# One decoder layer on one core: a re-ordered first phase, sample states updated in the MLP phase, and a fixed order for the last block

## The chip, the core and the metric

The kernel runs on one core of one Trainium2 chip. Every time is in device microseconds (us). The time of the kernel before is the median of three runs; the profile and the trace are those of one further execution of the same program.

## The reference

One step of one decoder layer (width 2048) is computed for two streams: a prompt of 256 tokens and 8 sample tokens that each carry recurrent states from the past. All arithmetic is float32.

```python
mod = silu(c) @ w_ada + b_ada                      # 6 x 2048 columns
h = rmsnorm(x, g_pre_mix) * (1 + sc1) + sh1
z = h @ w_in                                       # 2048 x 13328
# A: gMLP spatial gating; B: HGRN2, 8 heads of 128 x 128; C: GLA, 4 heads of 128 x 256
#    S_t = diag(f_t) S_{t-1} + k_t v_t^T ;  o_t = S_t^T q_t          (per head)
merged = sum over A, B, C of sigmoid(z_gate_n) * (y_n @ w_branch_n)
x = x + gt1 * rmsnorm(merged @ w_out, g_post_mix)
h2 = rmsnorm(x, g_pre_mlp) * (1 + sc2) + sh2
y2 = square(relu(h2 @ w_mlp_up)) @ w_mlp_down      # 2048 x 8192 x 2048
x = x + gt2 * rmsnorm(y2, g_post_mlp)
```

The outputs are both streams, the final recurrent states of the prompt, the updated states of the 8 samples (two sets of 4 MB) and the normalised v rows of branch A. A sample has one token, so its output row can be had from the new state, `o = S_new^T q`, or from the old one, `o = (q.k) v + S_old^T (q f)`; the new state must be written out in either case.

## The kernel before

**Tiles and products.** Prompt and samples lie side by side as 264 columns (NT), with the features on the partitions. A product in float32 is made of three TensorE matmuls: the weight block is split in `whi` (ScalarE, line 109) and the rest `wlo` (VectorE, line 106), the activations likewise, and lines 601, 602 and 603 are whi·xh, whi·xl and wlo·xh, each 128x128 against 128x264. A weight block of 512 KB makes 24 such matmuls; the text calls that a granule. There are 578 of them. `Stream` loads weight blocks five granules ahead through SyncE's queue and has them split two granules ahead; six `whi` and six `wlo` buffers go round.

**Phases.** (1) The first phase, granules 0 to 79, from about 28 us: the first columns of `w_in`, taken in five chunks of 2, 2, 4, 4 and 4 of the 16 row tiles, because the modulation of those tiles must itself be computed from `w_ada`. A table (`at`, `acts`) says after which granule a step is issued: the loads and the products of `w_ada` (line 273), `sums`, `rows` and `tiles`, which modulates two row tiles (lines 413 and 415) and splits them. Chunk 2 begins at granule 20. (2) The mixer phase, to about 850 us: the rest of `w_in` and the branch weights stream, and two sets of generators (branch A, the recurrences of the prompt, and the samples) issue small work between granules. Each runs until its `yield`; a rate says how many steps are taken at each granule. (3) `w_out` and the norms, to about 1165 us. (4) The MLP, 8 blocks of 1024 columns, each 4 `linear` of 4 granules up and 8 `linear` of 2 granules down, to 1920 us. (5) The end: the last norm, the residual and the stores.

**Samples.** `samples_r` runs for each of three groups of four heads (two HGRN2, one GLA). For each 256 KB of state it loads the state (`st`, GpSimd's queue, line 1073) and the v rows laid over all partitions (`vbc`, line 1079), ScalarE scales by the decay (line 1099), VectorE adds k·v (line 1101), GpSimd's queue writes the result (line 1102), and TensorE makes the output from the new state (line 640). The wait before ScalarE's step is for a number of granules (`FETCHED`) and so a guess of when the loads have landed.

**Order.** `manual_schedule` makes the named engines run their instructions in program order. Every engine is in it until the MLP; there only TensorE is, and a planner places the others.

## Time and profile before

| what | before |
|---|---|
| median of three runs | 1937.72 us (1937.01 to 1941.59) |
| the profiled execution, and its span | 1936.48 us, 1934.7 us |
| TensorE matmuls busy | 1900.5 us (98%) |
| VectorE busy | 1191.7 us (62%) |
| ScalarE busy | 996.9 us (52%) |
| GpSimd busy | 87.7 us (5%) |
| mean granted TensorE clock | 0.998 |
| read and written in HBM | 427.6 MB, 11.7 MB |

A busy time is the union of an engine's instructions, so a matmul that is pipelined behind another does not count twice. Durations of single matmuls (about 0.28 us) are longer than their spacing (about 0.12 us) for that reason. "Waits" name for every idle stretch of an engine the instruction or transfer that ended last before the waiting instruction began.

### The profile page before, as it was taken

How to read it: one execution, taken by the hardware profiler on the slowest of the kernel's cores; microseconds unless marked ns; L12 is line 12 of the kernel's file. 1: busy time of each engine (PE TensorE's matmuls, PEld its weight loads, DVE VectorE, ACT ScalarE, POOL GpSimd, SP SyncE). 2: the span in 40 equal slices, each digit the busy share in tenths (PEclk: the TensorE clock that was granted, in tenths of full speed). 3: DMA queues.
4: the chain of work that ended last, by engine and by line, in shares of the span. 5: the costliest groups of instructions: out<-in, count | busy, mean ns of one | idle time of the engine just before them, and what ended most of it. 6: DMA issues, size and time to landing. Idle time of an engine off the chain costs nothing.

```text
span 1934.7 us, 42322 instructions
## 1 busy us (share of the span) xinstructions
PE 1900.5 (98%) x17092; PEld 1811.2 (94%) x17092; DVE 1191.7 (62%) x2129; ACT 996.9 (52%) x1812; POOL 87.7 (5%) x144
## 2 busy tenths in 40 slices
PE   7999999998999999999999999999999999999998
PEld 5989999998999998999999999999999999999997
DVE  5666567685577695565555667545555555555666
ACT  4444354664666765544444566454444545454544
POOL 1000000001101112200000010000000000000000
PEclk9999999999999999999999999999999999999999
DMA  9986696777588678987777846776655556565563
GB/s 325 349 319 236 226 307 206 226 254 252 184 269 278 221 260 277 309 264 251 251 252 231 304 143 193 230 239 188 183 178 183 182 179 184 176 184 179 181 183 102
DMA packets 339380, 442.06 MB, mean 228 GB/s; under 512 B 14930, under 2 KB 281024, under 8 KB 339184
## 3 DMA queue, kind: packets, MB, share of 16 engines
q1 hardware_dynamic: 329120, 409.62, 65.6%
q0 software_dynamic: 8992, 28.48, 4.6%
q8 instruction: 134, 2.20, 0.4%
q10 hardware_dynamic: 1072, 1.25, 0.2%
q14 instruction: 62, 0.51, 0.1%
HBM read 427.60 MB, written 11.70 MB: 227 GB/s over the span
## 4 chain that ended last, share of the span: by engine, by line
PE 94%; DVE 2%; DMA 2%; ACT 1%; issue 1%; POOL 0%; SPq 0%; DVEq 0%; ACTq 0%
PE mm L601 29%; PE mm L602 28%; PE mm L603 28%; PE ada L341 3%; PE ada L273 2%; DMA vbc<-vs_d 1%; PE sm L633 1%; DVE wlo L106 1%; PE sm L845 1%; PE sm L640 0%; DMA st<-in_state_gla_dram 0%; DMA b<-in_x_prompt_dram 0%; DVE b L103 0%; DMA b<-in_w_ada_dram 0%; ACT b L109 0%
## 5 line engine op out<-in xcount | busy, mean ns | idle before, releaser
L601 PE MATMUL mm<-b,whi 128*128 128x264 f32 x4592 | 1318.1, 287 | 5.7 <-DVE b L103 2.9
L602 PE MATMUL mm<-b,whi 128*128 128x264 f32 x4592 | 1307.7, 285 | 1.4 <-DVE b L106 1.2
L603 PE MATMUL mm<-b,wlo 128*128 128x264 f32 x4592 | 1305.1, 284 | 3.1 <-DVE wlo L106 2.6
L106 DVE TENSOR_TENSOR wlo<-raw,whi 128x512 fp32r<-128x512 f32 x1136 | 770.3, 689 | 498.0 <-ACT whi L109 495.4
L109 ACT CAST whi<-raw 128x512 fp32r<-128x512 f32 x1132 | 692.3, 618 | 726.9 <-PE mm L602 648.2
L601 PEld LDWEIGHTS mm<-b,whi 128*128 128x128 f32 x4592 | 865.4, 188 | 49.2 <-issue 24.7
L603 PEld LDWEIGHTS mm<-b,wlo 128*128 128x128 f32 x4592 | 865.5, 188 | 3.7 <-DVE wlo L106 3.7
L602 PEld LDWEIGHTS mm<-b,whi 128*128 128x128 f32 x4592 | 865.5, 188 | 2.4 <-DVE b L106 1.3
L103 DVE TENSOR_TENSOR b<-b,mm 128x528 f32<-128x528 f32 (+1 forms) x137 | 95.7, 700 | 98.2 <-PE mm L603 98.2
L1101 DVE SCALAR_TENSOR_TENSOR st<-vbc,b,st 128x128 f32<-128x128 f32 (+1 forms) x96 | 34.2, 391 | 54.7 <-DMA vbc<-vs_d 49.8
L1099 ACT ACTIVATE st<-st,fs 128x128 f32<-128x128 f32 (+1 forms) x96 | 37.0, 430 | 58.7 <-DMA st<-in_state_hgrn_dram 32.5
L273 PE MATMUL ada<-b,cT 128*32 128x256 f32 (+1 forms) x640 | 34.7, 354 | 6.9 <-DMA b<-in_w_ada_dram 6.8
L341 PE MATMUL ada<-araw,cT 128*32 128x512 f32 x296 | 39.9, 601 | 0.0
L273 PEld LDWEIGHTS ada<-b,cT 128*32 128x32 f32 x640 | 17.8, 112 | 18.8 <-ACT b L234 6.1
L100 DVE TENSOR_TENSOR b<-b,b 128x512 f32<-128x512 f32 (+1 forms) x47 | 34.1, 742 | 1.4 <-ACT b L1209 0.9
L1102 POOL DMA_DIRECT2D out_dram<-st x32 | 23.5, 735 | 156.4 <-DVE st L1101 155.6
L341 PE MATMUL ada<-b,cT 128*32 128x512 f32 x216 | 25.8, 593 | 0.0
L106 DVE TENSOR_TENSOR b<-gt,b 128x528 fp32r<-128x528 f32 x32 | 22.7, 708 | 3.6 <-ACT whi L109 0.5
L106 DVE TENSOR_TENSOR b<-b 128x1024 f32<-128x1024 f32 (+1 forms) x24 | 24.3, 1018 | 0.0
L100 DVE TENSOR_TENSOR gt<-vt 128x528 f32<-128x528 f32 x32 | 22.5, 702 | 0.9 <-ACT vt L1729 0.9
L1735 ACT ACTIVATE b<-vt 128x528 fp32r<-128x528 f32 x32 | 20.7, 647 | 1.0
L341 PEld LDWEIGHTS ada<-b,cT 128*32 128x32 f32 x216 | 6.9, 110 | 15.1 <-issue 14.6
(385 smaller groups left out, 882.6 us busy)
## 6 DMA issues: line engine op xcount, KB each, us to landing
raw<-in_w_in_dram SPq DMA_DIRECT2D x232, 512.0 KB, 4.6
raw<-in_w_mlp_up_dram SPq DMA_DIRECT2D x128, 512.0 KB, 3.7
raw<-in_w_mlp_down_dram SPq DMA_DIRECT2D x128, 512.0 KB, 3.6
b<-in_w_ada_dram SPq DMA_DIRECT2D x102, 512.0 KB, 6.3
araw<-in_w_ada_dram SPq DMA_DIRECT2D x74, 512.0 KB, 5.4
raw<-in_w_branch_dram SPq DMA_DIRECT2D x48, 512.0 KB, 4.3
raw<-in_w_out_dram SPq DMA_DIRECT2D x32, 512.0 KB, 4.2
b<-in_w_ada_dram SPq DMA_DIRECT2D x32, 256.0 KB, 6.5
```

Source lines behind the costliest of these rows:

```text
L100: V.tensor_tensor(o, a, b, op=ALU.mult)
L103: V.tensor_tensor(o, a, b, op=ALU.add)
L106: V.tensor_tensor(o, a, b, op=ALU.subtract)
L109: S.copy(hi, src)
L273: T.matmul(acc[32 * j:32 * j + 32, 0:n], cT[:, k, :], w[:, n * j:n * j + n], start=k == 0, stop=k == KT - 1)
L341: T.matmul(self.acc[32 * j:32 * j + 32, :], cT[:, k, :], ws[j // 2][:, j % 2 * 512:j % 2 * 512 + 512], start=k == 0, stop=k == KT - 1)
L601: T.matmul(o, a, xh(k + j), start=first and j == 0, stop=False)
L602: T.matmul(o, a, xl(k + j), start=False, stop=False)
L603: T.matmul(o, b, xh(k + j), start=False, stop=last and j == n - 1)
L1099: S.activation(st[:, i, :], st[:, i, :], AF.Copy, scale=fs[:, h0 + i, b:b + 1])
L1101: V.scalar_tensor_tensor(st[:, i, :], v[:, i, :], k[:, h0 + i, NP + b:NP + b + 1], st[:, i, :], ALU.mult, ALU.add)
L1102: nc.gpsimd.dma_start(G.s_out(b, h0, nh), st)
```

## The change

**First phase.** The scaling of the fourth quad of x moves from before granule 0 to after granules 1 and 2. Both `wlo` subtractions of granule 0 come after the modulation of both tiles. The first two granules run by part (`granule_by_part`): the whi·xh matmuls of a tile row first, then whi·xl, then wlo·xh. Splitting is separated from `tiles` as `parted`; for chunk 2 it is issued one granule later, and both tiles of a pair are modulated by ScalarE (`light`). The `w_ada` products of chunk 2 are issued after granules 8, 10, 13 and 16 in place of 9, 11, 14 and 17, and its loads one granule earlier.

**Mixer.** `samples_r` no longer makes the new state. It loads the old one (every third time into a `vbc` buffer), and TensorE takes its product with q·f from the buffer as loaded. The term (q·k)v is made once for each group: v rows by one or two transposes, q·k by a product with ones, then one scaling by ScalarE. Decay and k are kept in a constant, `kept`.

**MLP.** A generator `states` reads every block of state again, with the v rows, and makes and writes the new state. Each of its half steps waits for a token, the first column of what was last evacuated from an accumulator (`paced`); GpSimd copies that column and the needed columns of `kept`, and ScalarE's and VectorE's update reads that copy. GpSimd's order is fixed in this phase too.

**End.** The last two output tiles of the last block have accumulators of their own (`za`, `zb`), TensorE, VectorE and ScalarE run in program order there, the identity products and the transposes stand between the last products, the sample rows are made by GpSimd, and the stores are shared out to the two queues differently.

```diff
-        while late:
+        for _ in range(n):
             mul(*late.pop(0))
...
-            if j % 2 == 0:
+            if j % 2 == 0 and not light:
                 V.tensor_scalar(dst[:, j, 0:NP], src[:, j, :], A[:, k, 0:1], B[:, k, 0:1], ALU.mult, ALU.add)
             else:
                 S.activation(dst[:, j, 0:NP], src[:, j, :], AF.Identity, scale=A[:, k, 0:1], bias=B[:, k, 0:1])
-            if one or j % 2 == 1:
-                js = slice(j, j + 1) if one else slice(j - 1, j + 1)
-                split(dst[:, js, :], hi[:, js, :], lo[:, js, :])
...
+            at(gs[-1] + 1 + k // 2, firsts[c].tiles, firsts[c].k0 + k, c == 2)
+            at(gs[-1] + (2 if c == 2 else 1) + k // 2, firsts[c].parted, firsts[c].k0 + k)
+    at(1, x_scaled, 1)
+    at(2, x_scaled, 1)
...
-        at(5 + 2 * b // 3, firsts[2].load, b)
+        at(4 + 2 * b // 3, firsts[2].load, b)
...
-    at_batches(2, (9, 11, 14, 17))
+    at_batches(2, (8, 10, 13, 16))
...
+    def granule_by_part(accs, xh, xl):
+        for x in (xh, xl):
+            for j in range(n):
+                products(0, x, j, ms)
+        for a in range(len(accs)):
+            for j in range(n):
+                products(1, xh, j, ms[2 * a:2 * a + 2])
...
-            st, v = ahead.pop(0)[0], vals.pop(0)[0]
-            for i in range(nh):
-                S.activation(st[:, i, :], st[:, i, :], AF.Copy, scale=fs[:, h0 + i, b:b + 1])
-            for i in range(nh):
-                V.scalar_tensor_tensor(st[:, i, :], v[:, i, :], k[:, h0 + i, NP + b:NP + b + 1], st[:, i, :], ALU.mult, ALU.add)
-            nc.gpsimd.dma_start(G.s_out(b, h0, nh), st)
-            sts.append(st)
+            yield lambda: now[0] >= ahead[0][1] + FETCHED
+            sts.append(ahead.pop(0)[0])
...
+    def states():
+        for n, (G, b, h) in enumerate(todo):
+            st, v = ahead.pop(0)
+            for half in range(2):
+                yield lambda: paced[0] is not None
+                token()
+                fk = tmp([P, 16], "sx")[:, 0:nh].rearrange("p (c i) -> p c i", c=2)
+                nc.gpsimd.tensor_copy(fk, kept[:, G.i].rearrange("p c (h b) -> p c h b", h=4)[:, :, h + hs[0]:h + hs[-1] + 1, b])
+                write()
+                for j, i in enumerate(hs):
+                    S.activation(st[:, i, :], st[:, i, :], AF.Copy, scale=fk[:, 0, j:j + 1])
+                    V.scalar_tensor_tensor(st[:, i, :], v[:, i, :], fk[:, 1, j:j + 1], st[:, i, :], ALU.mult, ALU.add)
+                if half == 0 and n + 1 < len(todo):
+                    fetch(*todo[n + 1])
+            done.append((G.s_out(b, h, nh), st))
...
+    za, zb = new_acc(), new_acc()
...
+    last_products(0, 0)
+    last_products(0, 1)
+    gated_tile(0)
+    add(sqacc, sqacc, sq[:, 0, :])
+    last_products(1, 0)
+    pt = sm()
+    rows_tile(0)
+    last_products(1, 1)
+    first_part(0)
+    gated_tile(1)
```

**VectorE where chunk 2 begins.** In the rows, `mm` is an accumulator that L103 (L104 after) adds up, `mod` and `A` the modulation, `b_276` the pair of row tiles, `b_1322` (`b_1282` after) the rest from its split, and the word behind "waits" names the engine waited for. Before:

```order
L103 TENSOR_TENSOR mod<-sm_1313,vec 128x2x9 x3
L479 SCALAR_TENSOR_TENSOR A_168<-mod,vec 128x36 [waits DVE_49]
L100 TENSOR_TENSOR b_276<-xsn_128,A_168 128x2x8 [waits DVE_49]
L103 TENSOR_TENSOR b_276<-b_276,mod 128x2x8 [waits DVE_49]
L413 TENSOR_SCALAR b_276<-b_276,A_168,mod 128x256
L106 TENSOR_TENSOR b_1322<-b_276,b_1321 128x528 [waits Activation_49]
L103 TENSOR_TENSOR b_869<-b_869,mm_1329 128x528 [waits PE_49]
L103 TENSOR_TENSOR b_869<-b_869,mm_1330 128x528 [waits PE_49]
```

After:

```order
L104 TENSOR_TENSOR mod<-sm_1273,vec 128x2x9 x3
L477 SCALAR_TENSOR_TENSOR A_168<-mod,vec 128x36 [waits DVE_49]
L101 TENSOR_TENSOR b_276<-xsn_128,A_168 128x2x8 [waits DVE_49]
L104 TENSOR_TENSOR b_276<-b_276,mod 128x2x8 [waits DVE_49]
L104 TENSOR_TENSOR b_819<-b_819,mm_1287 128x528 [waits PE_49]
L104 TENSOR_TENSOR b_819<-b_819,mm_1288 128x528 [waits PE_49]
L107 TENSOR_TENSOR wlo_1316<-raw_1137,whi_1315 128x512 [waits Activation_49]
L107 TENSOR_TENSOR wlo_1320<-raw_1139,whi_1319 128x512 [waits Activation_49]
L107 TENSOR_TENSOR b_1282<-b_276,b_1281 128x528 [waits Activation_49]
```

The modulation by VectorE (L413) is gone, and the subtraction that waits for ScalarE stands behind the two evacuations and two weight splits instead of ahead of them.

**GpSimd in the mixer phase.** `st` are state buffers, `vbc` the buffers for v rows, `vs_d` the v rows in memory. Before, from the first state load on:

```order
L1073 DMA st_5306<-in_state_hgrn_dram 128x4x128 [waits DMASW6_49]
L1079 DMA vbc_5308<-vs_d 128x512 [waits DMASW7_49]
L1102 DMA out_dram<-st_5023 128x4x128 [waits DMASW3_49,DMASW0_49,DVE_49]
L1073 DMA st_5460<-in_state_hgrn_dram 128x4x128 [waits DMASW1_49]
L1079 DMA vbc_5462<-vs_d 128x512 [waits DMASW5_49]
L1102 DMA out_dram<-st_5108 128x4x128 [waits DMASW4_49,DVE_49]
L1073 DMA st_5607<-in_state_hgrn_dram 128x4x128 [waits DMASW0_49,PE_49]
```

After:

```order
L1094 DMA st_5107<-in_state_hgrn_dram 128x4x128 [waits DMASW4_49]
L1101 MEMSET xsn_5110 128x128 [waits DVE_49]
L1094 DMA vbc_5588<-in_state_hgrn_dram 128x4x128 [waits DMASW5_49]
L1094 DMA st_5624<-in_state_hgrn_dram 128x4x128 [waits DMASW6_49]
L1094 DMA st_5660<-in_state_hgrn_dram 128x4x128 [waits DMASW7_49]
L1094 DMA vbc_5821<-in_state_hgrn_dram 128x4x128 [waits DMASW0_49]
L1094 DMA st_5869<-in_state_hgrn_dram 128x4x128 [waits DMASW3_49,DMASW1_49,PE_49]
```

The loads of v rows and the stores between the state loads are gone, and with them the waits for VectorE on this queue.

**ScalarE in the MLP phase after.** `whi` are the weight casts, L1360 the scaling of a state by the decay in `sx`:

```order
L110 CAST whi_17548<-raw_17447 128x512 [waits DMAHW6_49,DVE_49,PE_49]
L1360 ACTIVATE st_17252<-st_17252,sx_17560 128x128 [waits DMASW2_49,DMASW1_49,Pool_49]
L1360 ACTIVATE st_17252<-st_17252,sx_17560 128x128
L110 CAST whi_17552<-raw_17447 128x512 [waits DVE_49,PE_49]
L110 CAST whi_17595<-raw_17481 128x512 [waits DMAHW7_49,DVE_49,PE_49]
L110 CAST whi_17599<-raw_17481 128x512 [waits DVE_49,PE_49]
L1360 ACTIVATE st_17252<-st_17252,sx_17643 128x128 [waits Pool_49]
L1360 ACTIVATE st_17252<-st_17252,sx_17643 128x128
```

Two state scalings stand between weight casts for every two granules of the down products; the first of a block waits for two transfers and for GpSimd's copy, and the casts behind it wait with it.

## The prediction

> **What bounds the kernel now.** First the page, then stretches of 50 us, then TensorE's waits.

> ```profile
> span 1934.7 us, 42322 instructions
> PE 1900.5 (98%) x17092; PEld 1811.2 (94%) x17092; DVE 1191.7 (62%) x2129; ACT 996.9 (52%) x1812; POOL 87.7 (5%) x144
> ```

> ```profile
> 100.00:150.00 50.00, 46.06 (x419) 42.26 (x417) 31.23 (x66) 21.36 (x36) 0.00 (x0) 1.00 0.90 324
> 400.00:450.00 50.00, 50.00 (x769) 45.84 (x768) 34.94 (x68) 26.84 (x52) 8.12 (x12) 1.00 0.84 257
> 450.00:500.00 50.00, 44.23 (x409) 41.17 (x408) 27.46 (x52) 25.93 (x58) 5.27 (x8) 0.93 0.72 236
> 1400.00:1450.00 50.00, 50.00 (x413) 50.00 (x412) 27.88 (x41) 24.60 (x41) 0.00 (x0) 1.00 0.60 180
> ```

> The columns behind the stretch are the busy time of TensorE, its weight load, VectorE, ScalarE and GpSimd, then the clock, the DMA share and GB/s. TensorE bounds the kernel: 1900.5 of 1934.7 us, and in the MLP 413 matmuls in 50 us, 0.121 us each, without a gap. An edit can win only what lies in the other 34.2 us, and in stretches like 450 to 500, where the clock was 0.93. So the first question for each part is whether it touches a wait of TensorE.

> ```profile
> PE sm L1220 <- DVE b L100: 3.8, 1, 3.8
> PE mm L601 <- DVE b L103: 2.9, 3, 2.2
> PE mm L603 <- DVE wlo L106: 2.6, 4, 1.9
> PE mm L601 <- ACT b L109: 1.9, 2, 1.4
> PE sm L845 <- ACT gt L1422: 1.4, 1, 1.4
> ```

> These are total, number and longest. The longest of each lie in the mixer (3.8 and 1.9), where chunk 2 begins (2.2 and the 1.4 of L601) and at the end (the 1.4 of L845).

> **Mixer.** The chain of waits, and slices of 2 us, show where these two stalls come from.

> ```profile
> 444.45 10.45 DMA vbc<-vs_d
> 466.47 6.86 DMA vbc<-vs_d
> 476.35 0.64 ACT b L1207
> 477.01 0.70 DVE b L100
> 477.75 1.24 PE sm L1220 x8
> ```

> ```profile
> 458.00:460.00 2.00, 1.97 (x10) 1.67 (x9) 1.71 (x3) 2.00 (x7) 0.00 (x0) 0.56 0.85 253
> 460.00:462.00 2.00, 2.00 (x12) 2.00 (x11) 2.00 (x5) 1.46 (x4) 0.00 (x0) 0.59 0.25 28
> 478.00:480.00 2.00, 2.00 (x14) 2.00 (x14) 0.30 (x1) 0.58 (x1) 0.00 (x0) 0.68 1.03 328
> 480.00:482.00 2.00, 2.00 (x11) 2.00 (x10) 0.00 (x0) 0.55 (x1) 0.00 (x0) 0.50 0.84 272
> ```

> VectorE stands still until `vbc` lands, 10.45 and 6.86 us after issue, and the `wlo` subtractions and the exponent chain of the prompt stand behind it in order. TensorE pays the stall (1.9 and 3.8 us) and then runs at about half clock for 4 us: 10 and 12 products in 2 us after the first, where 2/0.121 = 16.5 would fit, and 0.68 and 0.50 after the second. By the clock that is 4 x (1 − 0.575) = 1.7 and 4 x (1 − 0.59) = 1.6 us, by the products 11 x 0.121 = 1.3 and (2.5 + 5.5) x 0.121 = 1.0. The row of the whole stretch gives the sum in another way: 50 − 44.23 = 5.8 us without a matmul and 50 x 0.07 = 3.5 us of clock, **9.3**. I take this as the gain; its low end is 1.9 + 3.8 + 1.3 + 1.0 = 8.0.

> The change removes the transfer of `vbc`, the scaling and the addition from this phase.

> ```profile
> L1101 DVE SCALAR_TENSOR_TENSOR st<-vbc,b,st 128x128 f32<-128x128 f32 (+1 forms) x96 | 34.2, 391 | 54.7 <-DMA vbc<-vs_d 49.8
> L1099 ACT ACTIVATE st<-st,fs 128x128 f32<-128x128 f32 (+1 forms) x96 | 37.0, 430 | 58.7 <-DMA st<-in_state_hgrn_dram 32.5
> vbc<-vs_d POOLq DMA_DIRECT2D x32, 256.0 KB, 6.5
> ```

> VectorE sat 54.7 us in front of L1101, 49.8 of them for `vbc`; neither it nor ScalarE waits for a state transfer there any more. TensorE itself does now: its products read the tile as landed. They are issued when four states of a sample are gathered and a slot is due; with `FETCHED` 4 granules of 2.9 us and the slot behind it a tile is at least 11.6 us old, and mostly over 20, against landings of 6.5 (the median of `vbc`, of the same size) and 10.45 (the longest on the chain). I put this wait at 0; at 10.45 it would still be 0.

> New on TensorE are four transposes and three one-column products. The nearest rows are in the last fence: 0.66 us for four transposes, 0.58 for four one-column products. 4 x 0.165 + 3 x 0.145 = 1.1 us, **−1.1**.

> **First phase.** VectorE, then ScalarE, then the weight load, where chunk 2 begins:

> ```profile
> 102.02 0.41 DVE L413 TENSOR_SCALAR b<-b,A,mod 128x256 f32<-128x256 f32 x1
> 103.17 0.71 DVE L106 TENSOR_TENSOR b<-b,b 128x528 fp32r<-128x528 f32 x1 [0.74 <-ACT b L109]
> 103.79 1.31 DVE L103 TENSOR_TENSOR b<-b,mm 128x528 f32<-128x528 f32 x2
> 107.02 0.63 ACT L109 CAST b<-b 128x528 fp32r<-128x528 f32 x1 [2.34 <-DVE b L413]
> 95.41 0.21 PEld L273 LDWEIGHTS ada<-b,cT 128*32 128x32 f32 x8 [0.22 <-DMA b<-in_w_ada_dram]
> ```

> The 2.2 us stall ends when L103 frees an accumulator at 104.64. From 102.02 to 103.79 the modulation, a wait and the split stand ahead of it; all three move behind it or to ScalarE, so L103 can start 1.77 us earlier: 1.8 us gained. The second stall (1.4) follows ScalarE's cast at 107.02, which waited 2.34 us for VectorE's modulation. ScalarE now does both tiles itself (0.60 more) and splits a granule later, so this one shrinks but does not vanish; between 0 and 1.4 I take 0.7. Against that, the `w_ada` products move a granule (2.9 us) forward. The last batch already waited 0.22 us for its load; the load is issued earlier too, but behind weight loads on SyncE's queue that wait for buffers, so it may gain anything from nothing to 2.9. Costs 0 to 2.9, bounds for lack of a row; half of the way, less what other work hides, I take 0.8. **1.8 + 0.7 − 0.8 = 1.7**, from −1.1 to 3.2.

> ```profile
> 28.79 0.39 PE L602 MATMUL mm<-b,whi 128*128 128x264 f32 x1 [0.51 <-DVE b L106]
> 35.01 0.39 PE L601 MATMUL mm<-b,whi 128*128 128x264 f32 x1 [0.53 <-DVE b L819]
> 30.65 1.28 DVE L100 TENSOR_TENSOR b<-sm,vt 128x512 f32<-128x512 f32 x2
> ```

> At the start whi·xh of eight matmuls (8 x 0.121 = 1.0 us) now covers the split that cost 0.51 us, and 1.28 us of scaling leaves VectorE ahead of the evacuation that cost 0.53. The `wlo` half now comes later in each granule and the next granule needs its accumulators sooner, so I do not take both in full: **0.8**, from 0.2 to 1.2.

> **MLP.** Here nothing waits today, so it can only cost.

> ```profile
> L109 ACT CAST whi<-raw 128x512 fp32r<-128x512 f32 x480 | 297.2, 619 | 369.7 <-PE mm L602 343.0 <-DVE wlo L106 26.7
> L106 DVE TENSOR_TENSOR wlo<-raw,whi 128x512 fp32r<-128x512 f32 x480 | 331.7, 691 | 286.5 <-ACT whi L109 286.5
> L1642 POOL CAST b<-xsn 128x32 fp32r<-128x32 f32 x4 | 2.0, 488 | 0.1
> L1102 POOL DMA_DIRECT2D out_dram<-st x32 | 23.5, 735 | 156.4 <-DVE st L1101 155.6
> ```

> 66 tokens, one for each `linear`, stretch the 32 updates over 5.4 of 8 blocks, some 525 us. ScalarE's 37.0 us make 3.5 more in each 50 us: 24.6 + 3.5 = 28.1; VectorE's 34.2 make 3.3: 27.9 + 3.3 = 31.2. Both stay far below 50. 32 loads, 32 `vbc` and 32 stores of 256 KB, 25 MB in 525 us, add 48 GB/s to 180, and the share goes from 0.60 to about 0.76, below the 0.84 of the mixer. About 130 copies by GpSimd at 0.488 us and the issues fit in its 5% use. What hides all this is the lead of the casts: ScalarE waits 343.0 of its 369.7 idle us for TensorE to free a `whi` buffer. Six buffers are three granules; a freed one is needed again two granules later (5.8 us), and cast plus subtraction take 1.3, which leaves 4.5. A block of state is fetched two tokens ahead, in down 2 x 2 x 24 x 0.121 = 11.6 us, less 3.2 for GpSimd's two copies (0.488) and three issues (0.735): 8.4 us, against 6.5 to 10.45 for landing. A late one holds ScalarE 2.1 us, inside the 4.5. I take **0**; without that cover each late load would stall TensorE as in the mixer, 3.7 us with the clock.

> [...]

> **End.**

> ```profile
> 1920.52 0.77 DVE L103 TENSOR_TENSOR b<-b,mm 128x264 f32<-128x264 f32 x2 [2.08 <-PE mm L603]
> 1921.92 0.66 PE L845 MATMUL sm<-cst,gt 128*128 128x128 f32 x4 [1.44 <-ACT gt L1422]
> 1922.79 0.58 PE L1460 MATMUL sm<-cst,a 128*128 128x1 f32 x4 [0.22 <-DVE a L103]
> 1924.88 1.41 DVE L1810 SCALAR_TENSOR_TENSOR b<-b,nr,b 128x512 f32<-128x512 f32 x2
> 1929.90 1.07 ACTq L1812 DMA_DIRECT2D out_dram<-b  x2
> ```

> After the last product only one tile's addition (0.38) and square (0.4) precede the norm's products, where two of each and a sum over tokens (L103, 0.43) preceded 1922.79: about 0.8 us. The last issues, at 1929.90 to 1930.97 in one queue, are shared by two: up to 0.5 more, of which the stores' own time (the span ends at 1934.7) may take some. **1.0**, from 0.5 to 1.3.

> **Sum.** 9.3 − 1.1 + 1.7 + 0.8 + 0 + 1.0 = 11.7 us. On the profiled 1936.48 that is 1924.8; the median shown, 1937.72, lies 1.24 higher, so **1926.0 us** for the median, 0.6% faster. All terms at their low ends, 8.0 − 1.1 − 1.1 + 0.2 + 0.5 = 6.5, give 1931.2; at their high ends, 9.3 − 1.1 + 3.2 + 1.2 + 1.3 = 13.9, give 1923.8. The waits of TensorE that I count nowhere are each under 0.6 us; a few of them gone would take the low end to 1920.

> **Rivals.** (a) The second mixer stall has a cause of its own: its chain runs through ScalarE's L1207 and VectorE's L100, which belong to the prompt's recurrence. For it speaks that they stand directly ahead of L1220; against it that 6.86 us of `vbc` stand ahead of them. Then 3.8 + 1.6 stay: 1931.4. (b) The first phase gains nothing, since the `w_ada` wait eats both its terms: 1926.0 + 2.5 = 1928.5. (c) The updates hold up the MLP. The place is the first ScalarE scaling of a state, which waits for two transfers with weight casts behind it. It decides from a landing of 8.4 + 4.5 = 12.9 us on, or where the planner puts the scaling ahead of casts that are due. Some 21 of the 32 fetches fall in the down products; at 3.7 us each, two late ones cost 7.4 (1933.4, no measurable change) and five cost 18.5, which is 6.8 more than the gain: 1944.5, slower. For it speaks 10.45 us of landing in the mixer, against it the lower DMA share and a ScalarE with 45% idle. (d) The change does not do what it says in the mixer: the stall moves to TensorE's own wait for `st`, since half of the loads now queue for buffers that only its products free; the same 9.3 us stay lost: 1935.3, no change. (e) The low clock after the first stall is not its doing: a wait of 2.2 us stands in the stretch 100 to 150 too, and the clock there was 1.00. Then its 1.7 us stay: 1927.7. Against it stands 0.56 right behind the stall.

> [...]

> **How the numbers follow.** Forecast 0.52; (a) 0.12, (b) 0.11, (c) 0.13, of which 0.10 slower and 0.03 without change, (d) 0.07, (e) 0.05. About 0.3%, 5.8 us, is what a measurement of this kernel can tell from no change; the border is at 1931.9. Faster: the forecast less a little of its slow end, (a) by two thirds (its 1931.4 is at the border), (b) and (e), 0.50 + 0.08 + 0.11 + 0.05 = 0.74. Same: 0.02 + 0.04 + 0.03 + 0.07 = 0.16. Slower: 0.10. The range of 1920 to 1936 holds the forecast, (a), (b), (d) and (e) and leaves out (c)'s slow side and what is faster than any term allows.

> **What would show it.** Right: no wait of L1220 and no stretch of clock under 0.9 between 450 and 490; waits of L601 below 2 us around 100 us; ScalarE near 28 and VectorE near 31 in the MLP's 50-us stretches, TensorE still 50.00 with 413; the last issue 1 us nearer to the last product. Wrong: waits of L603 or L601 for `wlo` or `whi` in the MLP, or of a product for `st`; a wait for `w_ada` of over 2 us near 92.

## The result, and the profile after

The changed kernel takes 1925.78 us in the median of six runs (1924.67 to 1926.84), against 1935.95 for the kernel before in its six (1933.97 to 1941.59). The ratio is 0.9945, with a 95% interval of 0.9934 to 0.9955. Between the medians lie 10.2 us, and the ratio makes it 10.6; the prediction had 11.7 and a median of 1926.0. A second set of runs of the same kernel gave 1924.33 us and 0.9941 (0.9929 to 0.9953). The profiled execution took 1926.15 us, 10.3 less than that of before.

The page of the changed kernel, its waits of TensorE, and the stretches shown of before:

```profile
span 1924.4 us, 42614 instructions
PE 1901.4 (99%) x17108; PEld 1813.0 (94%) x17108; DVE 1200.4 (62%) x2139; ACT 1007.3 (52%) x1821; POOL 154.9 (8%) x311
```

```profile
PE ada L274 <- DMA b<-in_w_ada_dram: 6.6, 2, 5.8
...
PE mm L599 <- DVE b L104: 1.3, 4, 0.4
PE mm L600 <- DVE b L107: 0.9, 2, 0.5
PE mm L599 <- ACT b L110: 0.8, 1, 0.8
PE sm L1651 <- ACT vt L1602: 0.6, 1, 0.6
```

```profile
100.00:150.00 50.00, 49.13 (x446) 45.54 (x446) 31.38 (x61) 23.21 (x40) 0.00 (x0) 1.00 0.89 325
450.00:500.00 50.00, 50.00 (x489) 47.70 (x489) 25.77 (x55) 28.17 (x66) 0.76 (x1) 1.00 0.61 186
1400.00:1450.00 50.00, 50.00 (x412) 50.00 (x411) 31.59 (x54) 28.24 (x52) 8.10 (x16) 1.00 0.72 220
```

TensorE's busy time is the same (1901.4 and 1900.5 us); the gain is idle time. The first row is the wait at the start that was there before (6.8 and 6.0). The waits of L1220's products and for a `wlo` are gone from the list, and 450 to 500 us has no gap and a clock of 1.00, where it had 44.23 us and 0.93. The spread has shrunk too: the changed kernel's eleven times lie within 3.2 us, 23 of the kernel before within 8.5. The MLP's row holds what was worked out: ScalarE 28.24 (28.1 was predicted), VectorE 31.59 (31.2), 220 GB/s (228), share 0.72 (0.76), and TensorE still 50.00. The updates stand there as groups, none of them ended by a transfer:

```profile
L1360 ACT ACTIVATE st<-st,sx 128x128 f32<-128x128 f32 (+1 forms) x96 | 39.3, 433 | 37.0 <-POOL sx L1357 37.0
L1361 DVE SCALAR_TENSOR_TENSOR st<-vbc,sx,st 128x128 f32<-128x128 f32 (+1 forms) x96 | 36.1, 394 | 28.7 <-ACT st L1360 28.7
L1339 POOL COPY sa<-vt 128x1 f32<-128x1 f32 x24 | 16.8, 699 | 301.5 <-ACT vt L1805 301.5
```

To see where the time went, the 1156 `wlo` subtractions of weights were numbered in each trace, and the starts of the same number compared with those of the kernel before. The table gives what each profile gained (us) between such marks; negative is lost. The marks lie at 57, 133, 881, 1130, 1232 and 1910 us of the kernel before.

| profile | to 57 | chunk 2, to 133 | mixer, to 881 | to 1130 | norms, to 1232 | MLP, to 1910 | end | total |
|---|---|---|---|---|---|---|---|---|
| changed | 0.1 | 2.7 | 9.9 | 0.4 | −1.8 | −1.6 | 0.6 | 10.3 |
| changed, second | 1.1 | 2.8 | 10.0 | 0.4 | −0.2 | −1.6 | 0.3 | 12.8 |
| without updates | 0.6 | 2.6 | 9.7 | 0.4 | −0.2 | −1.6 | 0.5 | 12.0 |
| updates moved alone | −0.9 | 0.0 | 9.4 | 0.1 | 0.1 | −0.6 | 0.0 | 8.0 |
| first phase alone | −0.3 | 2.7 | 2.4 | −0.3 | −0.1 | −1.9 | −1.1 | 1.5 |
| end alone | 0.2 | 0.0 | 2.4 | 0.0 | 0.0 | 0.0 | 0.6 | 3.1 |

The rows below the first are the experiments that follow. The first column moves by up to 1 us either way in kernels that do the same there: it holds the arrival of the first `w_ada` blocks. The −1.1 at the end of the first phase's kernel is not the work of an edit: its trace has half clock from 1921.61 us on for 3.41 us, among small products whose code is that of the kernel before.

### The profile page after: what moved, and what is told of

It reads as the page before. It is cut to its first block, busy times and chain, and to the rows that moved or that the text cites. A ratio compares the mean times of both kernels' runs of the same rounds, so it can differ in the third digit from the quotient of the medians.

```text
span 1924.4 us, 42614 instructions
## 1 busy us (share of the span) xinstructions
PE 1901.4 (99%) x17108; PEld 1813.0 (94%) x17108; DVE 1200.4 (62%) x2139; ACT 1007.3 (52%) x1821; POOL 154.9 (8%) x311
## 4 chain that ended last, share of the span: by engine, by line
PE 96%; DVE 1%; DMA 1%; ACT 1%; issue 0%; SPq 0%; ACTq 0%; DVEq 0%
PE mm L599 29%; PE mm L600 28%; PE mm L601 28%; PE ada L342 3%; PE ada L274 1%; PE sm L649 1%; DVE wlo L107 1%; PE sm L864 1%; DMA b<-in_w_ada_dram 1%; PE sm L656 1%; DMA b<-in_x_prompt_dram 0%; DMA raw<-in_w_in_dram 0%; DVE b L104 0%; PE sm L971 0%; PE sm L1317 0%
## 5 line engine op out<-in xcount | busy, mean ns | idle before, releaser
L599 PE MATMUL mm<-b,whi 128*128 128x264 f32 x4568 | 1311.2, 287 | 2.4 <-DVE b L104 1.3
L601 PE MATMUL mm<-b,wlo 128*128 128x264 f32 x4568 | 1296.8, 284 | 0.0
L599 PEld LDWEIGHTS mm<-b,whi 128*128 128x128 f32 x4568 | 859.9, 188 | 44.4 <-issue 27.8
L601 PEld LDWEIGHTS mm<-b,wlo 128*128 128x128 f32 x4568 | 859.1, 188 | 0.0
L104 DVE TENSOR_TENSOR b<-b,mm 128x528 f32<-128x528 f32 (+1 forms) x137 | 95.7, 700 | 97.5 <-PE mm L601 95.1
L1360 ACT ACTIVATE st<-st,sx 128x128 f32<-128x128 f32 (+1 forms) x96 | 39.3, 433 | 37.0 <-POOL sx L1357 37.0
L1361 DVE SCALAR_TENSOR_TENSOR st<-vbc,sx,st 128x128 f32<-128x128 f32 (+1 forms) x96 | 36.1, 394 | 28.7 <-ACT st L1360 28.7
L1339 POOL COPY sa<-vt 128x1 f32<-128x1 f32 x24 | 16.8, 699 | 301.5 <-ACT vt L1805 301.5
L274 PEld LDWEIGHTS ada<-b,cT 128*32 128x32 f32 x640 | 17.9, 114 | 19.0 <-ACT b L235 5.9
L1339 POOL COPY sa<-b 128x1 f32<-128x1 f32 x42 | 19.0, 452 | 179.1 <-DVE b L104 142.3
## 6 DMA issues: line engine op xcount, KB each, us to landing
b<-in_w_ada_dram SPq DMA_DIRECT2D x32, 256.0 KB, 6.6
```

What stands on the lines that cost most here:

```text
L104: V.tensor_tensor(o, a, b, op=ALU.add)
L274: T.matmul(acc[32 * j:32 * j + 32, 0:n], cT[:, k, :], w[:, n * j:n * j + n], start=k == 0, stop=k == KT - 1)
L599: T.matmul(o, a, xh(k + j), start=first and j == 0, stop=False)
L601: T.matmul(o, b, xh(k + j), start=False, stop=last and j == n - 1)
L1339: nc.gpsimd.tensor_copy(tmp([P, 16], "sa")[:, 0:1], paced[0])
L1360: S.activation(st[:, i, :], st[:, i, :], AF.Copy, scale=fk[:, 0, j:j + 1])
```

## The experiments

### The change in its parts

Each kernel is the kernel before with the hunks of one part of the diff: the first phase (`x_scaled`, `modulate`, `parted`, `granule_by_part`, the batches), or the move of the updates (`samples_r`, `kept`, `states`), or the end. In the last, the updates of the samples' states are left out of the changed kernel:

```diff
-    bs.g.append(states())
```

> The kernel before with the edits of the first phase alone. By the trace of the changed kernel, where the stream stood 0.1 us earlier behind granule 1 and 2.8 us earlier behind the start of chunk 2 and kept that to the mixer, the time falls by 2.8 us, to a ratio of 0.9985; nearly all of it at chunk 2, with waits of L599 for evacuations under 0.5 us there. By the prediction as written (0.8 at the start, 1.7 at chunk 2) it falls by 2.5, which the time cannot tell from 2.8 but the profile can: 0.8 us ahead by the end of granule 1. If the gain of the first phase needs the rest of the change, or is eaten later by the mixer's wait for v rows (which is set by transfers, not by TensorE), the ratio is 0.9995 to 1.000.

> The kernel before with the edits of the end alone. By the trace of the changed kernel the stretch from the last product's start to the end of the span is 13.7 in place of 14.5 us, less 0.2 for products that now stand between: 0.6 us gained, ratio 0.9997, too small for the times; the profile must show the rstd of the last norm some 3.8 us behind the start of the last product in place of 4.7. By the prediction it is 1.0 us.

> The kernel before with the move of the state update from the mixer to the MLP alone. If the mixer's two stalls were the wait for v rows and the update costs the MLP nothing, 9.3 - 1.1 = 8.2 us by the prediction, 9.9 by where the stream stands at the end of the mixer in the changed kernel: ratio 0.9949 to 0.9958, without any wait of L1220 (its line here differs) and without a wait of a weight product in the MLP. If the update costs the MLP the 1.6 us by which the changed kernel's stream fell back there in its profile, 8.3: 0.9957, and the time from the first to the last evacuation of the MLP is 1.6 us longer than in a kernel without the update. If the stall has a cause of its own in the prompt's recurrence, about 4 us: 0.998.

> The changed kernel without its updates in the MLP phase; the updated states of the samples are neither made nor written (left out). If the updates cost nothing on the path, the same time as the changed kernel (ratio to before 0.9945, between 0.9935 and 0.9955), and TensorE's spacing of products in the MLP as with the updates. If they cost the 1.6 us by which the changed kernel's stream fell back between 1220 and 1860 us, 0.9937, and the spacing of products is 0.1213 us as before in place of 0.1217 to 0.1222. If they cost more by way of the clock or of lost GpSimd time, below 0.993.

Measured, as ratios to the kernel before: first phase 0.999 (0.9981 to 0.9998), end 0.9985 (0.9975 to 0.9994), updates moved 0.9951 (0.9939 to 0.9963), changed kernel without updates 0.9934 (0.9922 to 0.9947).

The move of the updates carries the gain: 0.49% of 0.55%. The first phase shows its 2.7 us at chunk 2 in each of the table's profiles that have it. Its gain at the start is there too, though the table's first column hides it: from the start of the last `w_ada` product ahead of the stream to that of the stream's 73rd product it is 13.82 us in three profiles without the edits (before, updates moved, end) and 12.87 in three with them, 0.95 us. The interval of 0.999 reaches 3.7 us at its lower end, so time and profile agree, but the time alone would have shown neither part.

The end gained 0.6 us in its profile and 1.2 to 4.8 in the times. The profile bears out the small figure only: from the last product on the stretches differ by 0.6, and the other 2.4 us lie in the mixer, whose code is the same there. The 0.9997 that was expected lies outside the interval, and why the times fell by more is open.

That is the second finding. With the same mixer code, the end-alone and first-phase-alone profiles lose 2.4 us less there than the profile of before. The waits of the first of them, and two of its slices:

```profile
PE sm L1220 <- DVE b L100: 3.6, 1, 3.6
...
PE mm L603 <- DVE wlo L106: 1.2, 5, 0.3
```

```profile
450.00:500.00 50.00, 45.78 (x431) 42.50 (x430) 29.37 (x55) 27.65 (x63) 5.59 (x8) 0.97 0.72 239
476.00:478.00 2.00, 2.00 (x11) 2.00 (x11) 0.00 (x0) 0.58 (x1) 0.00 (x0) 0.50 1.08 397
```

The stall at L1220 is there each time, with half clock behind it. The other one, of 1.9 us in the profile of before, is 0.3 here and costs no clock. So the 9.3 us were read from the one of three profiles that lost most; beside the two others the move wins 9.9 − 2.4 = 7.5. Whether the 2.4 us differ from execution to execution or from program to program is not shown: the kernel before has one profile, and its 1936.48 us lie close to the median of 23 runs (1936.65).

The kernel without updates answers what they cost: TensorE's stream loses 1.58 us in the MLP with them and 1.58 without them. The updates cost nothing there. Its ratio is lower by 0.0011, inside both intervals, and its profile differs from the first of the changed kernel by 1.7 us in one place, the norms at 1130 us (below). The 1.6 us of the MLP are lost in other kernels too: 1.9 with the first phase alone, 0.6 with the moved updates, 0.0 with the end. They belong to no single edit, for of the kernels further down one that differs from the kernel before by a constant in the mixer loses 1.6 there (`FETCHED = 4`), and one that has the edits of the first phase and of the end loses 0.3. There is no wait in it, only the spacing of products: in stretches of 85 us between 1390 and 1815 us it is 0.1213 to 0.1219 us in the mean in the kernel before and 0.1216 to 0.1222 in the changed one. Why a product is slower there was not found.

### What the cover in the MLP is worth

The load of a state and its v rows is moved from two tokens ahead of use to one, and to none:

```diff
-                if half == 0 and n + 1 < len(todo):
+                if half == 1 and n + 1 < len(todo):
                     fetch(*todo[n + 1])
```

```diff
-        fetch(*todo[0])
...
-            st, v = ahead.pop(0)
...
                 token()
+                if half == 0:
+                    fetch(G, b, h)
+                    st, v = ahead.pop(0)
...
-                if half == 0 and n + 1 < len(todo):
-                    fetch(*todo[n + 1])
```

> The changed kernel with each state and its v rows loaded one token ahead of use in place of two. In the down products a token comes every 5.8 us; the loads are issued some 1.4 us behind theirs and used some 0.7 behind the next, 5.1 us later, against landings of 5.4 and 6.2 us in the median and 10.0 at most: ScalarE waits about 1 us for most and up to 5 for a few. By the prediction's cover of 4.5 us the time stays that of the changed kernel (0.9945, within 0.001), with waits of L1360 for transfers and none of TensorE. If there is no such cover, 21 loads late by 1 to 5 us cost 20 to 60 us: 1.005 or more.

> The changed kernel with each state and its v rows loaded at the token of their own use. ScalarE then waits for landing: 1.4 + 0.56 + about 6 us behind the token, less 0.7, some 7 us in each of 32 updates. By the cover of 4.5 us TensorE stalls 2.5 us each time, 80 us in all with little clock lost, 1.02 to 1.05 times the kernel before; with a cover of 7 or more nothing is lost; with none it is 7 x 32 = 220 us, 1.11.

One token ahead: 0.994 (0.9921 to 0.9958), the same as the changed kernel; ScalarE waits 4.5 us in all for transfers and TensorE not at all. At use: 1.0107 (1.0083 to 1.013), slower than the kernel before. ScalarE's groups there, between 1210 and 1790 us, and TensorE's longest wait:

```profile
L1361 ACT ACTIVATE st<-st,sx 128x128 f32<-128x128 f32 x64 | 22.7, 395 | 103.6 <-DMA st<-in_state_hgrn_dram 35.4 <-issue 29.5 <-POOL sx L1358 22.9
L1361 ACT ACTIVATE st<-st,sx 128x256 f32<-128x256 f32 x32 | 16.3, 509 | 100.2 <-DMA st<-in_state_gla_dram 41.5 <-POOL sx L1358 29.9 <-issue 28.8
```

```profile
PE mm L599 <- DVE b L104: 19.8, 16, 3.1
```

The stream loses 34.7 us in the MLP, 33.1 more than the changed kernel, 1.0 for each of 32 states; four stretches of 3.41 us at half clock are part of it. ScalarE stood 204 us ahead of its scalings, 6.4 for each state, where the changed kernel has 37. So the casts' lead covers some 5.4 us of such a wait, an estimate from these two means; the prediction had 4.5, and the expectation of 80 us was too high by more than twice. Rival (c) has its mechanism here, at 1.0 us for each state and not at 3.7, but the changed kernel is two tokens away from it.

### Is a late transfer all there is to the mixer's stalls?

If it is, an earlier transfer should do without the move. Two small edits of the kernel before, and one of them together with the first phase and the end:

```diff
-FETCHED = 3
+FETCHED = 4
```

```diff
+            if n + 1 < len(steps):
+                values(*steps[n + 1])
             if n + 2 < len(steps):
                 yield lambda: len(sts) + sum(len(x[3]) for x in samples) <= ST_BUFS - 3
                 fetch(*steps[n + 2])
-            if n + 1 < len(steps):
-                values(*steps[n + 1])
```

> The kernel before with one constant changed: its wait for loaded states is 4 granules and for the v rows 3 in place of 3 and 2, 8.8 in place of 5.9 us. If the mixer's stalls are no more than VectorE in order behind a transfer that has not landed, 2.9 us more of lead take most of them: the wait of L1220 (3.6 to 3.8 us in three profiles) falls under 1 us and its half clock goes with it, and the time falls by 4 to 6 us (ratio 0.997 to 0.998). If the stall has a cause of its own in the prompt's recurrence, the wait of L1220 stays over 3 us and the ratio is 0.9995 to 1.0005. What the move of the update wins over this constant is then the price of the move: states_only stood at 0.9951.

> The kernel before with the load of the v rows issued ahead of the load of the state that follows in the same step, and nothing else. In the kernel before the v rows stand on GpSimd's queue behind a state load that waits for TensorE to free a buffer (16 us of idle before the issue at 443.7), so they are issued at the last moment whatever the number of granules says; the constant of 4 granules made it worse for that reason. If this order is the cause of the stalls, the wait of VectorE for v rows (49.8 us in the kernel before) falls under 25 us, L1220's wait of 3.6 to 3.8 us under 1.5, and the ratio is 0.996 to 0.998. If the states themselves come as late as the v rows, ScalarE's wait for them takes the place and the ratio is 0.999 to 1.002. If the queue is not the cause, nothing changes.

> The kernel before with the edits of the first phase and of the end and with the v rows ahead, the update left in the mixer. If the v rows' place in the queue was the whole of the mixer's loss, it does without the 1.1 us of added products and without the second reading of the states: ratio 0.9940 to 0.9950, as fast as the changed kernel or 1 us faster. If the mixer's stalls stay, the first phase (3.7 us by the profiles) and the end (0.6) alone: 0.9975 to 0.9985. In between, by what values_first wins.

All three missed. The constant gave 1.0048 (1.0033 to 1.0063), the order 1.0019 (1.0011 to 1.0028), the combination 0.9992 (0.9984 to 1.0001). With the constant, TensorE's wait, the issues on GpSimd's queue ahead of it, and the transfer on the chain that ends in it:

```profile
PE sm L1220 <- DVE b L100: 7.9, 1, 7.9
```

```profile
440.48 0.75 POOL L1073 DMA_DIRECT2D st<-in_state_hgrn_dram  x1 [32.80 <-PE sm L640]
...
460.51 0.75 POOL L1073 DMA_DIRECT2D st<-in_state_hgrn_dram  x1 [11.71 <-PE sm L640]
461.25 0.55 POOL L1079 DMA_DIRECT2D vbc<-vs_d  x1
461.80 0.76 POOL L1102 DMA_DIRECT2D out_dram<-st  x1
462.55 0.75 POOL L1073 DMA_DIRECT2D st<-in_state_hgrn_dram  x1
```

```profile
462.55 8.13 DMA st<-in_state_hgrn_dram
```

The queue stands until TensorE's products on earlier states (L640) free a buffer, 32.80 and 11.71 us here; in the same stretch of the kernel before it stands 18.13 and 16.07 us. The granules that the constant counts pass while the queue stands; a longer count only pushes the whole chain, and L1220 behind it, later. Here it is the state itself that lands last, 8.13 us after its issue. With the v rows ahead of the state, VectorE's wait for them falls from 49.8 to 34.2 us and L1220's from 3.8 to 2.1, but other waits of 1.4 to 1.5 us come up in its place:

```profile
PE sm L1220 <- DVE b L100: 2.1, 1, 2.1
PE mm L603 <- DVE wlo L106: 1.9, 4, 1.0
...
PE sm L1242 <- ACT b L1233: 1.5, 1, 1.5
...
PE sm L633 <- DVE b L100: 1.4, 1, 1.4
```

This profile shows the mild end: its execution took 1935.89 us, the fastest of twelve with a median of 1939.43, so where the median loses its 3 us is not seen. ScalarE's wait for the states did not take the place, as the second branch of that expectation had it; it fell from 58.4 to 49.8 us. In the combination's profile the first phase and the end keep their 2.8 and 0.6 us, and the mixer loses 2.5 more than in the kernel before.

What remains by exclusion, and what the changed kernel bears out: the update in place ties four engines to four state buffers. TensorE frees a buffer, GpSimd loads, ScalarE and VectorE wait in order, TensorE waits for VectorE. The change takes ScalarE and VectorE out of this ring. Its loads have six buffers in place of four, but that did not clear the queue: GpSimd waits longer for TensorE ahead of its state loads (205 us, 134 before), and nobody waits for GpSimd. No run gave the kernel before more buffers, or took only the v rows out of it, so these parts of the move are not priced one by one.

### When a stall costs clock

Behind each of two outputs of a down block in the changed kernel, VectorE makes a copy (and, the second time, three products more), for which a small TensorE product waits:

```diff
+            if f < NFB - 1 and m in (2, 6):
+                probe = tmp([P, 2, NT], "gt")
+                V.tensor_copy(probe, dst)
+                for _ in range(0 if m == 2 else 3):
+                    mul(probe, probe, probe)
+                T.matmul(sm([P, 2]), ident, probe[:, 0, 0:2], start=True, stop=True)
```

> The changed kernel with 14 stalls put into TensorE's stream in the down products of the first seven blocks: seven short ones (a small product waits for the evacuation and one copy by VectorE, about 1.5 to 2 us) and seven long ones (three multiplications more, about 4 us). If a stall of any such length halves the clock, all 14 are followed by some 3 us of products at twice the spacing. [...] If the clock is judged in windows that run on by themselves, some of the short ones, by where they fall, and nearly all of the long ones.

This kernel ran once (1997.09 us). Three of the 14 stalls, and the clock around the first two, in slices of 3.41 us for a reason given below:

```profile
1265.04 0.38 PE L1839 MATMUL sm<-gt,cst 128*128 128x2 f32 x2 [1.66 <-DVE gt L1836]
1376.19 0.38 PE L1839 MATMUL sm<-gt,cst 128*128 128x2 f32 x2 [1.74 <-DVE gt L1836]
1404.95 0.58 PE L1839 MATMUL sm<-gt,cst 128*128 128x2 f32 x2 [4.85 <-DVE gt L101]
```

```profile
1262.37:1265.78 3.41, 1.75 (x15) 1.54 (x14) 1.89 (x4) 1.79 (x5) 0.60 (x2) 1.00 0.99 328
1265.78:1269.19 3.41, 3.41 (x17) 3.41 (x17) 1.17 (x3) 0.71 (x2) 0.00 (x0) 0.50 0.70 239
1269.19:1272.61 3.42, 3.42 (x30) 3.42 (x29) 1.30 (x2) 1.24 (x2) 0.00 (x0) 1.00 0.08 22
1371.60:1375.01 3.41, 2.85 (x24) 2.64 (x22) 2.38 (x4) 1.70 (x3) 0.49 (x1) 1.00 0.99 275
1375.01:1378.42 3.41, 2.23 (x18) 2.23 (x19) 1.77 (x5) 1.05 (x3) 0.86 (x2) 1.00 0.89 306
1378.42:1381.84 3.42, 3.42 (x30) 3.42 (x30) 1.58 (x3) 1.50 (x3) 0.00 (x0) 1.00 0.25 89
```

The first two stalls are alike, 1.66 and 1.74 us; behind one the clock is 0.50, behind the other 1.00. Of the seven short stalls three were followed by half clock, of the seven long ones (4.3 to 5.2 us from product to product) all seven. Half clock lasts 3.41 us behind a short stall, which loses 1.7 us, and 6.83 behind a long one.

The first mixer stall of the kernel before was of that kind: the window up to 458.22 has 1.50 us of matmuls and 1.91 without, and the next one is at half clock.

```profile
454.81:458.22 3.41, 1.50 (x12) 1.42 (x12) 3.20 (x7) 1.11 (x3) 0.00 (x0) 1.00 0.18 35
458.22:461.63 3.41, 3.38 (x16) 3.08 (x16) 3.17 (x6) 2.87 (x8) 0.00 (x0) 0.50 0.50 149
```

> The changed kernel once more, unchanged, beside the two above and for a second profile. If the 1.7 us that the stream lost at 1130 to 1140 us in the first profile is a matter of where the clock's windows fall, the times spread over some 2 us in two groups and this profile may have no stretch at half clock there, with a span of 1922.7 to 1923.2; if it belongs to the kernel, the stretch is there again at the same place and the span is 1924.4.

The same happens without an experiment in the norms, where for some 2.5 us TensorE has only thin products. The changed kernel's first profile, then its second, behind the same products:

```profile
1133.00:1135.00 2.00, 2.00 (x16) 0.44 (x8) 1.79 (x13) 1.29 (x5) 0.97 (x3) 0.50 0.02 4
1135.00:1137.00 2.00, 2.00 (x16) 0.57 (x12) 1.78 (x8) 1.58 (x4) 0.92 (x2) 0.65 0.35 37
```

```profile
1132.00:1134.00 2.00, 2.00 (x24) 0.61 (x20) 1.79 (x12) 1.18 (x4) 1.07 (x3) 1.00 0.01 4
1134.00:1136.00 2.00, 2.00 (x22) 0.56 (x15) 1.75 (x7) 1.61 (x4) 0.87 (x3) 1.00 0.81 227
```

The same instructions ran at 0.50 once and at 1.00 once, and the spans were 1924.4 and 1921.9 us; 1.6 of the 2.5 us between them lie here, and 1.0 in the arrival of the first loads. The second span is below the 1922.7 expected for that second reason. The kernel with the v rows ahead lost 1.7 us at this place as well, the other ten profiles of the table and the experiments at most 0.2. It is chance and no part of the change. Here the window ahead of the half clock, from 1129.57 us, had only 0.56 us without a matmul. One in the kernel before, from 1140.89 us, had 0.56 too and was followed by full clock; only its last 1.2 us were thin products, where the other has 2.5 us of them. Idle time alone does not decide here, then; whether thin products count for less, no run shows.

## Why the prediction was right

The median was forecast at 1926.0 and came out at 1925.8. That it fits to 0.2 us is luck: the gain is 10.2 us and not 11.7, and the median of before from which it was taken fell from 1937.72 with three runs to 1935.95 with six. The place and the mechanism of the gain were right. By its own steps:

**Start, 0.8.** 0.95 by the stretch behind the last `w_ada` product. Right, though in the changed kernel's profile the first loads came 0.9 us later and took it back.

**Chunk 2, 1.7.** 2.7. The term that was off is the `w_ada` wait, put at 0.8:

```profile
92.46 0.16 PEld L274 LDWEIGHTS ada<-b,cT 128*32 128x32 f32 x8 [0.35 <-DMA b<-in_w_ada_dram]
```

It went from 0.22 to 0.35 us, so the earlier issue kept step with the earlier use. The rest is the 1.9 of VectorE's order, whose wait went from 2.22 to 0.36 us, and the 1.0 of ScalarE's. Rival (b) is out.

**Mixer, 9.3 − 1.1.** 9.9 and 10.0 in two profiles, against the profile of before. The mechanism was right: with `vbc` out of VectorE's way, both stalls and their clock went, and (a) and (d) fell: no wait of L1220, and no wait of a product for a state. The idle time of TensorE in the mixer fell from 7.2 to 0.6 us, and its 3.4 us of lost clock went, 10.0 in sum. So 0.8 us of gain came from small waits that were counted nowhere, and the 1.1 us of new products do not show: that term was too high by about 1 us. Two readings in it were too firm. The first stall was taken as a property of the kernel, and two other profiles of the same mixer code lose 2.4 us less. And the clock of 0.56 behind the stall at 458 was set against the 1.00 at 100 us without a reason why the two differ. By the windows in the traces, 1.91 us of idle in one were enough at 458, and the stall of 2.2 us at 100 was cut by a boundary at 103.24 into parts that left at most 1.71 us of idle in one window. So (e) is out, and its sign at 100 us was a matter of place. The lateness of `vbc` was described and its cause not asked for; the queue behind a full set of buffers is the part that the prediction did not see.

**MLP, 0.** 0 for the updates, as the kernel without them shows. Their cover is some 5.4 us and not 4.5. But the stream fell back by 1.6 us there, with the updates and without them, for a reason that no step named and no run found.

**End, 1.0.** 0.3 to 0.6. The norm's factor came as forecast, 0.8 us sooner behind the last product, and the last issue was 1.5 sooner; the transfers took it back, as the prediction had allowed:

```profile
1914.32 0.17 DVE L200 SCALAR_TENSOR_TENSOR nr<-sa,nr 128x10 f32<-128x10 f32 x1
1919.55 0.36 SPq L1964 DMA_DIRECT2D out_dram<-xsn  x1
```

From the end of that issue to the end of the span it is 4.5 us, where it was 3.7 (1934.7 − 1930.97).

**The sum.** The terms that were too small (0.2 + 1.0 + 1.7) and those that were too large or missing (0.4 to 0.7 at the end, 1.6 in the MLP, 1.8 of clock in the norms in that profile) nearly cancel, and that is luck. The total is right to 1.5 us and the terms to 2.

## What to carry to other kernels

When VectorE updates a buffer that TensorE will read and free, and the loads for it stand on one queue, look for the ring that they make before moving a load forward: a longer count or another order in that ring moved the stall about, and taking ScalarE and VectorE out of it removed it. A phase with TensorE at 100% and 45% of ScalarE idle took such work for nothing, as long as its data were there a few microseconds early; here one `linear` ahead was enough and none ahead cost 33 us. Where short stalls decide, one profile is one draw: of two stalls of 1.66 and 1.74 us the one cost 1.7 us of clock and the other none, by where they fell, so compare the same stage over several profiles before a term of 2 us is believed.

## What was not expected of the hardware

A copy of one column by GpSimd took 0.18, 0.51 or 0.74 us, by what VectorE was doing. GpSimd, then VectorE, in the changed kernel's MLP:

```profile
1271.28 0.18 POOL L1339 COPY sa<-b 128x1 f32<-128x1 f32 x1 [5.57 <-ACT b L1830]
1376.32 0.51 POOL L1339 COPY sa<-b 128x1 f32<-128x1 f32 x1 [3.23 <-DVE b L104]
1405.86 0.74 POOL L1339 COPY sa<-vt 128x1 f32<-128x1 f32 x1 [9.36 <-ACT vt L1805]
1406.55 0.18 POOL L1357 COPY sx<-kept 128x4 f32<-128x4 f32 x1
```

```profile
1270.68 0.69 DVE L107 TENSOR_TENSOR wlo<-raw,whi 128x512 fp32r<-128x512 f32 x1 [0.64 <-ACT whi L110]
1376.10 0.68 DVE L107 TENSOR_TENSOR wlo<-raw,whi 128x512 fp32r<-128x512 f32 x1
1405.86 0.70 DVE L101 TENSOR_TENSOR gt<-vt 128x528 f32<-128x528 f32 x1
```

At 1405.86 the copy starts with VectorE's square of the same tile, both released by the same ScalarE instruction, and ends just behind it, as 22 of the 24 copies of `vt` do. At 1376.32 it starts 0.2 us behind a `wlo` subtraction, ends with that, and takes 0.51 us, as in 34 of the 42 copies behind down products. At 1271.28 the subtraction is all but over, and the copy takes 0.18 us, as in all eight others. VectorE's instructions keep their 0.7 us. Only GpSimd's took longer, and why, no run shows. A shared tile is not the cause, for the `wlo` subtraction and the copy behind it share none.
